# Hybrid attention and delta-rule block on one core: norm weights spread by a matrix product, squares summed on VectorE, row factors computed earlier

## The chip, the cores and the metric

The kernel runs on one core of one Trainium2 chip. The metric is the device time of one execution in microseconds (us). The time before is the median of three executions. A core has a matrix engine (TensorE, in the profile PE, with its weight loads as PEld), VectorE (DVE), ScalarE (ACT), GpSimd (POOL) and SyncE (SP), which here only issues transfers.

## The reference

One decoder layer on 1024 tokens of 1024 channels, in float32. The input is normalised, projected to 9,232 columns, goes through two token mixers, and is added back.

```
def _rmsnorm(x, w):
    y = x * rsqrt(mean(x * x, axis=-1) + NORM_EPS)
    return y * w

h = _rmsnorm(x, norm_w)              # per token a factor, per channel a weight
proj = h @ w_in
... mixer A: dilated window attention, three groups, rotary positions
... mixer B: gated delta rule in chunks of 64
merged = sigmoid(gate_a) * y_a + sigmoid(gate_b) * y_b
x = x + merged @ w_out
out = _rmsnorm(x, final_norm_w)
```

The change touches only `h` of the first line, the way in which it is brought into the kernel's tiles, and the order in which this and the first two projections are done.

## The kernel before, in words

TensorE multiplies in float16. Every operand is held as two float16 parts, an upper part (`h_hi`, `whi`) and the rest (`h_lo`, `wlo`); a product is three matmuls: upper by upper, upper by rest, rest by upper. `h_hi` and `h_lo` hold the normalised input with the channel on the partitions: 8 blocks of 128 channels by 1024 tokens. ScalarE makes an upper part, VectorE then the rest. PSUM has 8 banks of 128 x 512 float32; `bank(tag, bufs)` takes one of them, with the tags "mm" (3), "S" (2), "G" (2) and "O" (1).

The start (lines 96 to 561) normalises the input and computes the first two units of 256 columns, the queries `q` and keys `k` of one attention set, at the same time. It treats the tokens in two ways:

- **Tokens 0 to 511, four row tiles `t` of 128 tokens** (`xt`, tokens on the partitions). `rstd_rows(t)` (line 443): ScalarE squares the two halves of a row tile and sums them, takes the root; VectorE inverts it. `scale_rows(t)` (453): two operations on VectorE multiply a half of the tile by the token's factor and by the norm weights, which must lie along the free axis and be the same on all 128 partitions. That is the tile `nwr` (line 102), 128 x 1024, loaded from memory ready-made (114). `turn_rows(t)` (458): eight transposes on TensorE against the identity. `split_rows` (464): ScalarE and VectorE write the two parts into `h_hi` and `h_lo`. `rows_product(ps, w, t, c)` (471): 24 matmuls of 128 columns for one row tile and one half of the channels, a "run of rows" in what follows.
- **Tokens 512 to 1023, two quarters of 256 tokens** (`xs[2]` the third, `xs[3]` the fourth; channels on the partitions). `add_squares` (398): ScalarE squares pieces of 128 x 512, and GpSimd adds them up (`eng = GP`): three additions of 128 x 512 and one of 128 x 256 for a quarter. `rstd(i, acc)` (411): TensorE sums over the partitions, ScalarE takes the root, VectorE inverts and puts the factors on a diagonal (`diag`, two 128 x 128 blocks). `spread(i)` (421): a product of ones with the diagonal puts each token's factor on all partitions, in PSUM. `scale_x` (426): four operations on VectorE for a half of the channels, times norm weight (`nw16`, one value a partition) and factor. `split_h` (431): upper part on ScalarE, rest on VectorE. `quarter` (437): 24 matmuls of 256 columns for one block of 128 columns and one quarter.

The identity and the norm weights with one value a partition are the first 136 columns of the constants `cons`, which have a transfer of their own (116). All first loads are issued on SP's queue, in the order in which they are written (lines 112 to 116, then 483 to 492): x of row tile 0, the norm weights, the constants, the weight blocks of q, row tiles 1 and 2, the other constants, the weight blocks of k, row tile 3, the two quarters.

What sets the order: TensorE executes in the order of the program text throughout. In the block from line 495 to 559 VectorE and ScalarE also keep the order in which their instructions are written, among themselves. A scheduler may put instructions of later lines between them; it does so with the copies of `q` and `k` out of PSUM (`rope_evict`, line 599, "rx" in the profile), with the rotary products that follow (`rope_half`, 603) and with a small split (904). After the block `rope_first` (from line 656) goes on with the third quarter for `k` and the fourth for `q` and `k`. The block's second half before the change is shown at the end of this section, from line 526.

Of the kernel before, what the change touches and what calls it, by code (L numbers as in the profile page):

```python
# [19 lines left out]
D = 1024  # L20
# [57 lines left out]
def hybrid_block(ctx: ExitStack, tc: tile.TileContext, A):  # L78
# [3 lines left out]
    def STT(out, in0, scalar, in1, op0, op1, eng=None):  # L82
        (eng or V).scalar_tensor_tensor(out, in0, scalar, in1, op0=op0, op1=op1)  # L83
# [15 lines left out]
    spr = start[1].enter_context(tc.tile_pool(name="startr", bufs=1, side="right"))  # L99
    xt = sp.tile([128, 4, D], F32, name="xt")  # L100
    xs = {i: spr.tile([128, KT, 256], F32, name=f"xs{i}") for i in (2, 3)}
    nwr = spr.tile([128, D], F32, name="nwr")

    def load_xt(t, c):
        cs = slice(512 * c, 512 * c + 512)
# [2 lines left out]
    def load_x(i):  # L108
        for c in range(2):
            nc.sync.dma_start(out=xs[i][:, 4 * c:4 * c + 4], in_=A["xT"][i - 2, :, 4 * c:4 * c + 4])  # L110

    for c in range(2):
        load_xt(0, c)
    nc.sync.dma_start(out=nwr, in_=A["nwr"])
    cons = base.tile([128, A["cons"].shape[1]], F32, name="cons")
    nc.sync.dma_start(out=cons[:, :128 + KT], in_=A["cons"][:, :128 + KT])
    off = [0]

    def part(n):
# [276 lines left out]
    diag = base.tile([128, 2, 128], F32, name="diag", tag="diag", bufs=1)  # L396

    def add_squares(i, acc, c):
        eng = GP
        for k in (4 * c, 4 * c + 2):  # L400
            dst = acc if k == 0 else sp.tile([128, 2, 256], F32, name="sq", tag="sq", bufs=2)
            SC.activation(dst, xs[i][:, k:k + 2], AF.Square)
            if k:
                TT(acc, acc, dst, ALU.add, eng)
        if c:
            TT(acc[:, 0], acc[:, 0], acc[:, 1], ALU.add, eng)
# [24 lines left out]
    def split_h(i, c, n=4):  # L431
        for k in range(4 * c, 4 * c + 4, n):
            x, hl = xs[i][:, k:k + n], [h[:, k:k + n, i * 256:i * 256 + 256] for h in (h_hi, h_lo)]
            SC.copy(hl[0], x)  # L434
            TT(hl[1], x, hl[0], ALU.subtract)
# [7 lines left out]
    def rstd_rows(t):  # L443

        for c in range(2):
            junk = sp.tile([128, 2, 256], F32, name="sq", tag="sq", bufs=2).rearrange("p a b -> p (a b)")
            SC.activation(junk, xt[:, t, 512 * c:512 * c + 512], AF.Square, accum_out=ss[:, 2 * t + c:2 * t + c + 1])
        s0, s1 = ss[:, 2 * t:2 * t + 1], ss[:, 2 * t + 1:2 * t + 2]
        SC.activation(s0, s0, AF.Identity, bias=epsc, scale=1.0 / D)
        SC.activation(s1, s1, AF.Sqrt, bias=s0, scale=1.0 / D)  # L450
        V.reciprocal(s1, s1)

    def scale_rows(t):
        for c in range(2):
            x, n = xt[:, t, 512 * c:512 * c + 512], nwr[:, 512 * c:512 * c + 512]
            STT(x, x, ss[:, 2 * t + 1:2 * t + 2], n, ALU.mult, ALU.mult)

    def turn_rows(t):
        pts = [bank("G", 2), bank("G", 2)]
# [35 lines left out]
    with tc.manual_schedule(engines={nc.vector.engine, nc.scalar.engine}):  # L495
        wq, wk = w_first
        q, k = qk
        rstd_rows(0)
        scale_rows(0)
        pts = turn_rows(0)  # L500
        V.tensor_scalar(wq[0][:, 0:4], stage[0], W_SCALE, None, op0=ALU.mult)
        split_rows(0, pts, (0,))
        w_lo(stage[0], *wq, 0)
        split_rows(0, pts, (1,))
        rows_product(q, wq, 0, 0)
        w_hi(stage[1], wq[0], 1)
        w_lo(stage[1], *wq, 1)
        rows_product(q, wq, 0, 1)
        for t in (1, 2):
            rstd_rows(t)  # L510
            scale_rows(t)
        pts = turn_rows(1)
        split_rows(1, pts)
        rows_product(q, wq, 1, 0)
        pts = turn_rows(2)
        rows_product(q, wq, 1, 1)
        w_hi(stage[2], wk[0], 0)
        w_lo(stage[2], *wk, 0)
        split_rows(2, pts)
        w_hi(stage[3], wk[0], 1)  # L520
        w_lo(stage[3], *wk, 1)
        rstd_rows(3)
        scale_rows(3)
        for c in range(2):
            rows_product(q, wq, 2, c)
        for t in range(2):
            rows_product(k, wk, t, 0)
        pts = turn_rows(3)
        acc = [new_acc(0), new_acc(1)]
        for i in (2, 3):  # L530
            for c in range(2):
                add_squares(i, acc[i - 2], c)
            if i == 2:
                split_rows(3, pts)
        for t in range(2):
            rows_product(k, wk, t, 1)
        rstd(2, acc[0])
        for c in range(2):
            rows_product(k, wk, 2, c)
        pb = spread(2)  # L540
        scale_x(2, pb, 0)
        split_h(2, 0)
        for c in range(2):
            rows_product(q, wq, 3, c)
        rstd(3, acc[1])
        scale_x(2, pb, 1)
        split_h(2, 1)
        for c in range(2):
            rows_product(k, wk, 3, c)
        pb = spread(3)  # L550
        for c in range(2):
            scale_x(3, pb, c)
            split_h(3, c)
        V.tensor_copy(hide_b, hide64)
        V.tensor_copy(ident_b, ident)
        V.tensor_scalar(cw, convw, 0.5 * P_SCALE, None, op0=ALU.mult)
        q = [bank("mm", 3), bank("O", 1)]
        for ct in range(2):
            quarter(q[ct], wq, ct, 2)
# [1379 lines left out]
def _layout(x, norm_w, w_in, conv_w, a_log, dt_bias, gdn_norm_w, w_up_a, w_up_b, w_out, final_norm_w):  # L1939
    c = np.ascontiguousarray  # L1940
    x, w_in = np.asarray(x)[0], np.asarray(w_in)[0]
    cons, tabs, amask = _constants()
    rows = lambda v: np.broadcast_to(np.asarray(v).reshape(1, -1), (128, np.asarray(v).size))
    cons = np.concatenate([
        np.eye(128, dtype=np.float32),
        np.asarray(norm_w)[0].reshape(KT, 128).T,
        cons,
        np.asarray(conv_w)[0].reshape(4, 12, 128).transpose(2, 1, 0).reshape(128, 48),
        rows(np.asarray(a_log)[0]),
        rows(np.asarray(dt_bias)[0]),  # L1950
        np.tile(np.asarray(gdn_norm_w)[0], 2).reshape(128, 1),
    ], axis=1)
    wk = w_in.reshape(KT, 128, -1)
    w = np.stack([wk[:, :, cols].transpose(1, 0, 2) for cols in _columns()])
    up = np.concatenate([np.asarray(w_up_a)[0], np.asarray(w_up_b)[0]], axis=0)
    unit = lambda m: m.reshape(KT, 128, 4, 256).transpose(2, 1, 0, 3)
    return {
        "xT": c(x.T.reshape(KT, 128, 4, 256).transpose(2, 1, 0, 3)[2:]),
        "x": c(x),
        "cons": c(cons),  # L1960
        "nwr": c(rows(norm_w)),
        "tabs": tabs,
        "amask": amask,
        "w": c(w),
        "w7": c(np.stack([_seven(w[u]) for u in SEVENS])),
        "w_ba": c(wk[:, :, 7168:7184].transpose(1, 0, 2)),
        "w_up": c(unit(up)),
        "w_out": c(np.asarray(w_out)[0].reshape(2, 4, 128, 2, 512).transpose(1, 2, 0, 3, 4).reshape(4, 128, 4, 512)),
        "fnw": c(rows(final_norm_w)),
    }  # L1970
# [15 lines left out]
```

## Time and profile before

| | |
|---|---|
| median of 3 executions | 1087.89 us (1086.54, 1087.89, 1089.79) |
| span of the profiled execution | 1083.1 us |
| mean granted TensorE clock | 0.996 |
| busy PE, DVE, ACT, POOL | 1052.6, 854.9, 559.6, 66.5 us |

The time of the profiled execution itself is not listed; its span goes from the first to the last instruction and lies 4.8 us under the median. In ten-microsecond windows of the opening (busy time of each engine with its number of instructions, the granted clock, the share of the transfer engines, GB/s):

```
0.00:10.00 10.00, 2.30 (x12) 1.88 (x13) 2.83 (x8) 4.32 (x10) 0.20 (x4) 1.00 0.76 249
10.00:20.00 10.00, 8.57 (x109) 7.65 (x108) 9.32 (x15) 8.24 (x20) 0.68 (x1) 1.00 0.89 292
20.00:30.00 10.00, 10.00 (x172) 9.99 (x170) 4.58 (x7) 7.26 (x17) 6.77 (x7) 1.00 0.66 259
30.00:40.00 10.00, 10.00 (x156) 9.61 (x154) 5.70 (x13) 5.42 (x8) 3.24 (x3) 1.00 0.28 100
40.00:50.00 10.00, 8.15 (x59) 6.38 (x57) 8.77 (x14) 3.49 (x5) 0.57 (x1) 0.83 0.19 62
50.00:60.00 10.00, 10.00 (x95) 8.96 (x93) 7.25 (x12) 3.56 (x4) 0.00 (x0) 1.00 0.00 0
```

The columns are PE, PEld, DVE, ACT and POOL. TensorE's busy time counts a matmul from its start to its modelled end, and matmuls overlap. A line such as "L86" names a line of the kernel; L83 and L86 are two helpers (`STT` and `TT`) through which most of VectorE's work goes, so the tile names tell the operations apart.

### The profile page before, as it was taken

How to read it: one execution, taken by the hardware profiler on the slowest of the kernel's cores; microseconds unless marked ns; L12 is line 12 of the kernel's file. 1: busy time of each engine (PE TensorE's matmuls, PEld its weight loads, DVE VectorE, ACT ScalarE, POOL GpSimd, SP SyncE). 2: the span in 40 equal slices, each digit the busy share in tenths (PEclk: the TensorE clock that was granted, in tenths of full speed). 3: DMA queues.
4: the chain of work that ended last, by engine and by line, in shares of the span. 5: the costliest groups of instructions: out<-in, count | busy, mean ns of one | idle time of the engine just before them, and what ended most of it. 6: DMA issues, size and time to landing. Idle time of an engine off the chain costs nothing.

```text
span 1083.1 us, 23724 instructions
## 1 busy us (share of the span) xinstructions
PE 1052.6 (97%) x9426; PEld 641.4 (59%) x9426; DVE 854.9 (79%) x1967; ACT 559.6 (52%) x1272; POOL 66.5 (6%) x115
## 2 busy tenths in 40 slices
PE   6999999999999999999999999999999999999997
PEld 6894595775966855765645544555545554444443
DVE  5697897878879778979965797976588778799934
ACT  6445766667666565557645534244454345333622
POOL 1200000000000000000000000110200000000000
PEclk9999999999999999999999999999999999999999
DMA  8135531632724431741233457785685523753232
GB/s 295 60 98 136 128 109 55 167 99 66 190 79 132 101 126 47 182 117 59 75 122 136 111 130 175 250 247 159 195 269 167 147 99 101 285 185 123 83 120 78
DMA packets 99632, 148.99 MB, mean 138 GB/s; under 512 B 31152, under 2 KB 64432, under 8 KB 98368
## 3 DMA queue, kind: packets, MB, share of 16 engines
q1 hardware_dynamic: 69264, 85.20, 27.3%
q0 software_dynamic: 12320, 44.11, 13.5%
q10 hardware_dynamic: 17936, 18.16, 4.9%
q8 instruction: 74, 1.21, 0.5%
q14 instruction: 38, 0.31, 0.1%
HBM read 91.66 MB, written 36.90 MB: 119 GB/s over the span
## 4 chain that ended last, share of the span: by engine, by line
PE 59%; DVE 26%; DMA 5%; ACT 4%; issue 3%; SPq 2%; ACTq 0%; DVEq 0%
PE ps_mm L182 14%; PE ps_mm L184 14%; PE ps_mm L183 14%; DVE ca L83 4%; DVE wlo L83 2%; DVE X L86 2%; DVE stmp L86 2%; DVE sm L794 2%; DVE rt L86 2%; PE ps_S L182 1%; PE ps_S L184 1%; PE ps_S L183 1%; DVE tl L86 1%; PE ps_G L808 1%; SPq L624 1%
## 5 line engine op out<-in xcount | busy, mean ns | idle before, releaser
L184 PE MATMUL ps_mm<-h_hi,wlo 128*128 128x512 f16 (+1 forms) x552 | 208.6, 378 | 1.2 <-issue 1.2
L183 PE MATMUL ps_mm<-h_lo,whi 128*128 128x512 f16 (+1 forms) x492 | 185.9, 378 | 1.0 <-DVE h_lo L86 1.0
L182 PE MATMUL ps_mm<-h_hi,whi 128*128 128x512 f16 (+1 forms) x492 | 186.0, 378 | 0.9 <-ACT h_hi L434 0.9
L184 PEld LDWEIGHTS <-wlo 128*128 128x128 f16 x788 | 77.5, 98 | 89.5 <-issue 3.4
L182 PEld LDWEIGHTS <-whi 128*128 128x128 f16 x848 | 83.4, 98 | 70.8 <-issue 0.5
L183 PEld LDWEIGHTS <-whi 128*128 128x128 f16 x848 | 83.4, 98 | 69.1 <-issue 2.2
L182 PE MATMUL ps_mm<-whi,h_hi 128*128 128x256 f16 x384 | 105.1, 274 | 0.0
L798 ACT ACTIVATE sm<-sm,osb 128x128 f32<-128x128 f32 (+1 forms) x160 | 69.5, 435 | 68.7 <-DVE osb L794 62.0
L184 PE MATMUL ps_mm<-whi,h_lo 128*128 128x256 f16 x384 | 104.7, 273 | 0.0
L183 PE MATMUL ps_mm<-wlo,h_hi 128*128 128x256 f16 x384 | 104.7, 273 | 0.0
L86 DVE TENSOR_TENSOR tl<-ps_G,th 128x256 f16<-128x256 f32 (+1 forms) x96 | 51.8, 540 | 21.5 <-ACT th L813 21.0
L794 DVE CUSTOM_DVE_ANT_0 sm<-ps_S,amask 128x128 f32<-128x128 f32 (+1 forms) x192 | 59.2, 345 | 8.5 <-PE ps_S L787 8.3
L83 DVE SCALAR_TENSOR_TENSOR wlo<-wstage,whi 128x1024 f16<-128x1024 f32 x50 | 60.8, 1218 | 4.4 <-ACT whi L165 4.1
L83 DVE SCALAR_TENSOR_TENSOR ca<-xc,cw,ca 128x512 f32<-128x512 f32 x72 | 53.7, 746 | 7.1 <-ACT ca L1001 6.3
L165 ACT ACTIVATE whi<-wstage 128x1024 f16<-128x1024 f32 x49 | 51.3, 1051 | 3.0 <-PE ps_O L183 1.4
L83 DVE SCALAR_TENSOR_TENSOR whi<-wstage,whi 128x512 f16<-128x512 f32 x60 | 40.8, 687 | 13.6 <-ACT whi L329 12.9
L808 PE MATMUL ps_G<-cons,sm 128*128 128x128 f32 x280 | 47.5, 275 | 2.1 <-ACT sm L798 1.0
L183 PEld LDWEIGHTS <-h_hi 128*128 128x128 f16 x384 | 45.8, 119 | 1.6
L329 ACT ACTIVATE whi<-wstage 128x512 f16<-128x512 f32 x60 | 37.1, 626 | 18.5 <-DVE wstage L328 13.4
L182 PE MATMUL ps_mm<-h_hi,wlo 128*128 128x512 f16 x120 | 45.6, 380 | 1.0 <-DVE rx L83 1.0
L182 PEld LDWEIGHTS <-h_hi 128*128 128x128 f16 x384 | 45.5, 119 | 1.5
L184 PEld LDWEIGHTS <-h_lo 128*128 128x128 f16 x384 | 45.5, 119 | 1.5
(436 smaller groups left out, 2584.4 us busy)
## 6 DMA issues: line engine op xcount, KB each, us to landing
wstage<-in_w POOLq DMA_DIRECT2D x68, 512.0 KB, 4.8
og<-osb ACTq DMA_DIRECT2D x32, 132.0 KB, 2.2
og<-og SPq DMA_DIRECT2D x32, 132.0 KB, 2.2
gspb<-gst ACTq DMA_DIRECT2D x16, 256.0 KB, 2.3
sga<-gspa SPq DMA_DIRECT2D x8, 512.0 KB, 6.9
wstage<-in_w_up POOLq DMA_DIRECT2D x8, 512.0 KB, 5.1
wos<-in_w_out SPq DMA_DIRECT2D x8, 512.0 KB, 5.4
sgb<-gspb SPq DMA_DIRECT2D x8, 512.0 KB, 5.9
```

Source lines behind the costliest of these rows:

```text
L83: (eng or V).scalar_tensor_tensor(out, in0, scalar, in1, op0=op0, op1=op1)
L86: (eng or V).tensor_tensor(out, in0, in1, op)
L165: in_turn(SC.activation(hi[:, 4 * c:4 * c + 4], st, AF.Copy, scale=W_SCALE))
L182: PE.matmul(out, lhsT=wh(k), rhs=mh(k), start=first and i == 0, stop=False, skip_group_check=True)
L183: PE.matmul(out, lhsT=wh(k), rhs=ml(k), start=False, stop=False, skip_group_check=True)
L184: last_pe[0] = PE.matmul(out, lhsT=wl(k), rhs=mh(k), start=False, stop=last and i == len(ks) - 1, skip_group_check=True).ins.name
L329: in_turn(SC.activation(t[:, b, 0], self.part[name], AF.Copy, scale=W_SCALE))
L624: nc.sync.dma_start(out=dst[r0:r0 + 32, hd], in_=pt[name[1]][32 * hd:32 * hd + 32, "AB".index(name[0])])
L794: V.tensor_tensor_reduce(P[:, u, :128 * nk], psc[:, u * 256:u * 256 + 128 * nk], mask, -cexp, -NEG, ALU.add, ALU.min, accum_out=osb[:, 256 ...
L798: SC.activation(P[:, u, :128 * nk], P[:, u, :128 * nk], AF.Exp, bias=osb[:, 256 + hd:257 + hd], scale=-1.0, accum_out=osb[:, 260 + hd:261 ...
L808: PE.transpose(pt[:, c:c + 128], P[:, u, i * 128:i * 128 + 128], ident)
```

## The change

Three things are changed, all in the start.

1. The norm weights are not loaded as a tile of 128 equal rows. The constants (identity and one weight a partition) are loaded first and on ScalarE's queue. VectorE multiplies the identity by the weights (`nwd`, eight diagonal blocks), and TensorE multiplies a tile of ones by it, which gives the weights on all partitions in two PSUM banks; `scale_rows` reads them there.
2. The sums of squares of the third and fourth quarter are added on VectorE instead of GpSimd.
3. In the block's second half the order of TensorE, VectorE and ScalarE is rewritten: the factors of the third quarter are made after one run of rows of `k` (before: two), those of the fourth ahead of the last runs of rows of `q` (before: behind them), and the third quarter is scaled as a whole before the fourth's factors and split as a whole behind them.

```
-    nwr = spr.tile([128, D], F32, name="nwr")
+    nwd = spr.tile([128, KT, 128], F32, name="nwd")
+    ones0 = spr.tile([128, 128], F32, name="ones0")
+    V.memset(ones0, 1.0)
...
+    cons = base.tile([128, A["cons"].shape[1]], F32, name="cons")
+    nc.scalar.dma_start(out=cons[:, :128 + KT], in_=A["cons"][:, :128 + KT])
     for c in range(2):
         load_xt(0, c)
-    nc.sync.dma_start(out=nwr, in_=A["nwr"])
-    cons = base.tile([128, A["cons"].shape[1]], F32, name="cons")
-    nc.sync.dma_start(out=cons[:, :128 + KT], in_=A["cons"][:, :128 + KT])
...
     def add_squares(i, acc, c):
-        eng = GP
+        eng = V
...
     def scale_rows(t):
         for c in range(2):
-            x, n = xt[:, t, 512 * c:512 * c + 512], nwr[:, 512 * c:512 * c + 512]
-            STT(x, x, ss[:, 2 * t + 1:2 * t + 2], n, ALU.mult, ALU.mult)
+            x = xt[:, t, 512 * c:512 * c + 512]
+            STT(x, x, ss[:, 2 * t + 1:2 * t + 2], nwr[c], ALU.mult, ALU.mult)
...
         q, k = qk
+        TT(nwd, ident[:, None, :].to_broadcast([128, KT, 128]), normw[:, :, None].to_broadcast([128, KT, 128]), ALU.mult)
+        nwr = [bank("mm", 3), bank("O", 1)]
+        for c in range(2):
+            PE.matmul(nwr[c], lhsT=ones0, rhs=nwd[:, 4 * c:4 * c + 4].rearrange("p a b -> p (a b)"), start=True, stop=True)
         rstd_rows(0)
...
         acc = [new_acc(0), new_acc(1)]
-        for i in (2, 3):
-            for c in range(2):
-                add_squares(i, acc[i - 2], c)
-            if i == 2:
-                split_rows(3, pts)
-        for t in range(2):
-            rows_product(k, wk, t, 1)
+        for c in range(2):
+            add_squares(2, acc[0], c)
+        split_rows(3, pts)
+        rows_product(k, wk, 0, 1)
         rstd(2, acc[0])
         for c in range(2):
-            rows_product(k, wk, 2, c)
+            add_squares(3, acc[1], c)
+        rows_product(k, wk, 1, 1)
         pb = spread(2)
         scale_x(2, pb, 0)
-        split_h(2, 0)
+        rows_product(k, wk, 2, 0)
+        scale_x(2, pb, 1)
+        rows_product(k, wk, 2, 1)
+        rstd(3, acc[1])
+        for c in range(2):
+            split_h(2, c)
         for c in range(2):
             rows_product(q, wq, 3, c)
-        rstd(3, acc[1])
-        scale_x(2, pb, 1)
-        split_h(2, 1)
+        pb = spread(3)
         for c in range(2):
             rows_product(k, wk, 3, c)
-        pb = spread(3)
         for c in range(2):
             scale_x(3, pb, c)
             split_h(3, c)
```

More of the change, by code (lines that the diff above doesn't have):

```diff
@@ L1960, in _layout @@
         "cons": c(cons),
-        "nwr": c(rows(norm_w)),
         "tabs": tabs,
```

## The prediction

> **What bounds the kernel now.** I read the page first, then the waits of the opening 45 us, then the timeline of two places, then windows around the second.
>
> ```profile
> span 1083.1 us, 23724 instructions
> PE 1052.6 (97%) x9426; PEld 641.4 (59%) x9426; DVE 854.9 (79%) x1967; ACT 559.6 (52%) x1272; POOL 66.5 (6%) x115
> ```
>
> TensorE is the bound, idle for only 1083.1 - 1052.6 = 30.5 us. An edit of the opening counts only by what it does to TensorE's own idle or slow time, and what it saves there stays saved as long as TensorE's later waits move along. The waits of the first 45 us (engine, line, whom it waited for; total, times, longest):
>
> ```profile
> PE ps_G L461 <- DVE xt L83: 8.1, 2, 7.7
> PE ps_mm L183 <- DVE h_lo L86: 1.0, 1, 1.0
> PE ps_mm L477 <- DVE h_lo L83: 1.0, 1, 1.0
> PE ps_mm L182 <- ACT h_hi L434: 0.9, 1, 0.9
> ```
>
> Two places: the start, up to 7.7 us, and a hole of 0.9 + 1.0 us at some later point. The change touches both. The start in the timeline (start, duration, engine, line, tile; in brackets the idle time before and what ended it):
>
> ```profile
> 0.74 0.86 SPq L106 DMA_DIRECT2D xt<-in_x  x2
> ...
> 3.43 0.63 ACT L447 ACTIVATE sq<-xt 128x512 f32<-128x512 f32 x1 [1.20 <-DMA xt<-in_x]
> 6.14 0.16 DVE L451 RECIPROCAL ss<-ss 128x1 f32<-128x1 f32 x1 [5.24 <-ACT ss L450]
> 6.88 0.75 DVE L83 SCALAR_TENSOR_TENSOR xt<-xt,ss,nwr 128x512 f32<-128x512 f32 x1 [0.57 <-DMA nwr<-in_nwr]
> 7.54 0.16 DVE L147 TENSOR_SCALAR nw<-cons 128x8 f32<-128x8 f32 x1
> 7.62 0.74 DVE L83 SCALAR_TENSOR_TENSOR xt<-xt,ss,nwr 128x512 f32<-128x512 f32 x1
> 7.68 1.97 PE L461 MATMUL ps_G<-cons,xt 128*128 128x128 f32 x8 [7.68 <-DVE xt L83]
> 8.91 0.69 DVE L501 TENSOR_SCALAR whi<-wstage 128x1024 f16<-128x1024 f32 x1 [0.55 <-DMA wstage<-in_w]
> ...
> 17.04 0.61 PE L477 MATMUL ps_mm<-h_lo,whi 128*128 128x128 f16 x8 [0.98 <-DVE h_lo L83]
> ...
> 17.93 1.04 PE L461 MATMUL ps_G<-cons,xt 128*128 128x128 f32 x8
> ```
>
> The row factor is ready at 6.14 + 0.16 = 6.30, but the first scaling starts at 6.88: 0.57 us are lost to the loaded norm weights, and 0.55 us more to the first weight block at 8.91. The first eight transposes take 1.97 us, the same eight at 17.93 take 1.04: TensorE begins at about half speed. From 17.04 on it runs without a hole until the second place:
>
> ```profile
> 22.56 1.41 DVE L83 SCALAR_TENSOR_TENSOR xt<-xt,ss,nwr 128x512 f32<-128x512 f32 x2
> ...
> 23.45 4.35 POOL L86 TENSOR_TENSOR xt<-xt,sq 128x512 f32<-128x512 f32 x3 [0.75 <-ACT sq L402]
> ...
> 26.78 1.29 DVE L83 SCALAR_TENSOR_TENSOR h_lo<-ps_G,h_hi 128x512 f16<-128x512 f32 x2 [2.81 <-ACT h_hi L468]
> ...
> 28.57 4.03 POOL L86 TENSOR_TENSOR xt<-xt,sq 128x512 f32<-128x512 f32 x3
> ...
> 32.67 0.73 POOL L86 TENSOR_TENSOR xt<-xt 128x256 f32<-128x256 f32 x1
> ...
> 35.33 0.56 PE L414 MATMUL ps_G<-cons,xt 128*128 128x1 f32 x4
> ...
> 35.93 0.26 ACT L417 ACTIVATE rr<-ps_G,epsc 128x2 f32<-128x2 f32 x1 [0.34 <-PE ps_G L414]
> ...
> 36.09 1.97 ACT L599 COPY rx<-ps_mm 128x512 f32<-128x512 f32 x2
> ...
> 36.95 0.42 DVE L86 TENSOR_TENSOR diag<-cons,rr 128x256 f32<-128x256 f32 x1
> ...
> 37.30 1.65 DVE L83 SCALAR_TENSOR_TENSOR xs<-xs,nw,ps_G 128x256 f32<-128x256 f32 x4
> ...
> 38.43 0.65 PE L423 MATMUL ps_G<-diag,cons 128*128 128x256 f32 x2
> ...
> 38.91 0.27 PE L182 MATMUL ps_mm<-h_hi,whi 128*128 128x256 f16 x1
> ...
> 40.14 1.05 ACT L434 CAST h_hi<-xs 128x1024 f16<-128x1024 f32 x1
> ...
> 41.23 1.22 DVE L86 TENSOR_TENSOR h_lo<-xs,h_hi 128x1024 f16<-128x1024 f32 x1 [2.28 <-ACT h_hi L434]
> ...
> 47.99 0.27 PE L182 MATMUL ps_S<-h_hi,whi 128*128 128x256 f16 x1
> ...
> 53.23 0.27 PE L182 MATMUL ps_mm<-h_hi,whi 128*128 128x256 f16 x1
> ```
>
> The 48 matmuls of the query columns on the third quarter start at 38.91, the next 48 (key columns) at 47.99, the next at 53.23. The same work took 9.08 us and then 5.24 us, so the hole costs 3.84 us, not 1.9. Its cause: the upper half of the third quarter is scaled on VectorE (37.30) only after the factors of the fourth, and ScalarE copies q and k out of PSUM (36.09 and after) before it splits that half (40.14); VectorE's rest follows at 41.23. The other half of the cost is clock (busy time per engine and count, the granted clock, DMA):
>
> ```profile
> 39.19:42.60 3.41, 1.56 (x13) 1.11 (x12) 1.37 (x2) 2.21 (x4) 0.00 (x0) 1.00 0.28 115
> 42.60:46.01 3.41, 3.41 (x18) 2.42 (x18) 3.41 (x7) 1.04 (x1) 0.57 (x1) 0.50 0.10 18
> 104.07:107.48 3.41, 3.41 (x13) 1.48 (x11) 1.50 (x5) 1.44 (x8) 0.00 (x0) 0.50 0.00 0
> ```
>
> After a stretch with TensorE busy 1.56 of 3.41 us the clock is 0.50 for 3.41 us, which costs 1.71 us. So the hole is 3.84 - 1.71 = 2.13 us of waiting and 1.71 us of slow clock.
>
> **The change, part by part.** *Norm weights by a product.* Removed: a 512 KB load and two issues on SP (weights and constants), so the weight blocks behind them are issued about 0.9 us earlier. The constants now go out first, on ScalarE's queue, ahead of a table load and a tiny activation, which have room: ScalarE's first real work is at 3.43. Added: VectorE's memset and one 128x1024 product with the identity (the 128x1024 TENSOR_TENSOR at 41.23: 1.22 us), both in VectorE's 5.24 us of idle time; two f32 products of 512 columns on TensorE. From the 128x256 product at 38.43 to the next matmul is 0.48 us, so 512 columns cost some 0.9 us, and at the cold start twice that, about 1.8.
>
> When the constants land, no row shows. The nearest is the first block of x, issued in the same place and landed by 3.43; the far bound is the same constants on SP:
>
> ```profile
> cons<-in_cons SPq DMA_DIRECT2D x1, 68.0 KB, 4.8
> ```
>
> that is, 0.74 + 4.8 = 5.5. I take 3.4, since the block of x has the same position at the head of a queue. Then 3.4 + 0.16 + 1.22 = 4.8, the first product done at about 6.65, the second at 8.4. The first scaling starts at 6.65 instead of 6.88, but the second at 8.45 instead of 7.62, and VectorE's queue is in order: the weight rounding queued behind it (8.91 now) goes at about 9.2, whatever the earlier landing of the weights. TensorE is warm sooner, by about 8.5, so the transposes of the second half take half the time, and ScalarE's split of it stays in its place within 0.1. From there VectorE's chain to 17.04 is unchanged. I estimate the start at +0.2 us: the two waits of 0.57 and 0.55 are gone, and the second product is late in their place. Bounds: -0.6 (products in time; then the transposes limit) to +2.2 (landing at 5.5).
>
> *Sums on VectorE.* Removed from POOL: two sets of 4.35 or 4.03 us plus 0.73. Added to VectorE: six 128x512 additions and two of 128x256.
>
> ```profile
> L86 DVE TENSOR_TENSOR rt<-rt,rx 128x512 f32<-128x512 f32 x4 | 2.6, 688 | 0.0
> 29.62 2.70 PE ps_S L477 x48
> ```
>
> (a group by shape with its mean in ns; and a piece of the chain: two runs of rows take 2.70 us, one 1.35.) Issued back to back an addition takes about 0.65, so a quarter costs 3 x 0.65 + 0.4 = 2.35 us instead of about 5, in VectorE's idle time between 24 and 41. The first sum is queued ahead of the split of the last rows (26.78); it runs from 23.97 to about 26.4, before that split can start, so it delays nothing.
>
> *Factors ahead of other runs.* The new order, followed at these durations without the start's shift:
> - the third quarter's sum at 26.4; its factor on TensorE at 27.75 (behind one run of rows), ScalarE 0.6 later as between 35.33 and 35.93, VectorE's diagonal done by 29.4;
> - the spreading product at 29.5; the fourth quarter's sum on VectorE until about 32.0; then both halves of the third quarter's scaling, 2 x 1.65, until 35.3; the fourth's reciprocal and diagonal until 36.0;
> - TensorE meanwhile: two runs to 32.65, the fourth's factor to 33.05, two runs to 35.75; then it waits for the diagonal: 0.3 us, the one wait added, with the last runs of rows queued behind it;
> - spread to 36.5, two runs to 39.25. The third quarter's splits: ScalarE at 33.75 and 35.35, VectorE's rests done at 37.2 and 38.4, so both halves stand before 39.25, and the 48 matmuls run in 5.24.
>
> The key columns thus start at 39.25 + 5.24 = 44.5 instead of 47.99: -3.5; with +0.2 from the start -3.3. If q is copied out ahead of the upper half's split (2 x 0.98), that half is whole at about 40.1, and its first matmul is due after 12 of the 48, at 39.25 + 5.24 / 4 = 40.55: still covered; with k's copies also in front (two more of the kind) the old hole is back. The fourth quarter is due two runs of 48 later, at 49.7; on VectorE two scalings of 1.65, two rests of 1.22 and two rotation steps of 1.22 between them take it from 38.4 to about 47. What is late next is this (a row of the timeline, then one of all waits):
>
> ```profile
> 58.56 1.06 ACT L165 ACTIVATE whi<-wstage 128x1024 f16<-128x1024 f32 x1 [1.38 <-PE ps_O L183]
> ```
> ```profile
> PE ps_S L787 <- DMA Ql<-Ql: 2.3, 1, 2.3
> ```
>
> That wait ends a line of weight rounding, rotations and transfers. It begins at 58.56, where ScalarE waited 1.38 us until TensorE had done with the query weights, so it moves with TensorE and the gain is kept.
>
> *How often the slow stretch counts.* The two slow stretches begin 104.07 - 42.60 = 61.47 us apart, 18 times 3.41: they lie on a grid of 3.41 us. If the grid lies elsewhere, a hole of 2.1 us can fall across a line of it with both sides more than half busy, and no slow stretch follows. The three times before spread by 3.25 us, about two such prices, so I count the first stretch at 0.6 of 1.71, that is 1.0. [...]
>
> The sum for the median: -(2.13 - 0.3) + 0.2 - 1.0 = -2.6 us. The profiled execution's own time is not listed; its span lies 4.8 us below the median of 1087.89, and I apply the difference to that: 1085.3.
>
> **The rivals.**
> 1. *The slow stretch was in every execution*: -3.3, 1084.6. For it: the profile has it. Against: the spread of the times.
> 2. *The constants land before 3 us*: the start gives up to 0.6, in all -3.2 to -3.9, about 1084.4.
> 3. *A new wait in place of the old*: VectorE's longer queue makes the fourth's diagonal late by 1.5 to 2 us instead of 0.3, or the constants land near 5.5; about -0.7, 1087.2. Against it: VectorE's additions wait on nothing but ScalarE's squares.
> 4. *Slower*: q and k are in SBUF earlier relative to VectorE, and the instruction order may put the whole rotation of both (8 operations of about 1.22, 9.8 us) ahead of the fourth quarter's scaling at 38.4. Its first half would come at about 52 instead of 49.7: a 2 to 3 us hole, 1.7 of slow clock, and another wait for the second half, +4.5 against -2.6: about +1.9, 1089.8. It decides from some 3 us of rotation put ahead. Against it: today a rotation step goes in only where VectorE waits for ScalarE.
> 5. *Nothing changes*, because VectorE or DMA sets the pace after 58 us: 1087.9. Against it: TensorE's 97%.
>
> **How the numbers follow.** Forecast 0.50, rival 1 0.17, rival 2 0.09, rival 3 0.11, rival 4 0.08, rival 5 0.05. A change of 0.3%, 3.3 us, is about what a measurement can tell. The forecast's own spread (the stretch's share from 0 to 1, the start from -0.4 to +0.6) reaches from 1084.0 to 1086.8; a quarter of it lies beyond -3.3 (0.13), with two thirds of rival 1 (0.11) and most of rival 2 (0.07). I add 0.07 for the later instruction order, which is laid out anew behind the start and may fall better as well as worse: faster 0.38; slower by 0.3% needs rival 4 at its worst or the late landing together with it, and the same later order falling worse: 0.09. The range, 1083.2 to 1088.2, leaves out rival 4 and the best of rival 2.
>
> **What would show it.** Right: no TensorE wait of 0.9 us near 41 and clock 1.00 from 40 to 47; the key columns of the third quarter starting near 44.7 and 5.24 us before the next; POOL without additions; a TensorE wait under 0.6 for the diagonal; scalings of the first rows near 6.65 and 8.45. Wrong: the second scaling before 7.6 or after 9.5, ScalarE's four copies ahead of the upper half's split, a new TensorE wait before 60 us, or the saving at 50 us gone by 110 us.

## The result, and the profile after

Twenty-two executions of each kernel (those of before include the three that were known): before 1083.88 us (1078.52 to 1089.79), after 1079.57 us (1076.72 to 1083.70). The ratio is 0.9959 [0.9947, 0.9971], that is -4.4 us with an interval from -5.7 to -3.1. The kernel is faster by 0.41%, where the forecast was -2.6 us, under 0.3%. The 1085.3 us of the forecast lie 5.7 us above the measured median for two reasons: by the medians the change gave 1.7 us more than forecast, and the median of the three known executions of before (1087.89) lay 4.0 us above the median of 22.

The profiled execution after took 1077.67 us, with a mean granted clock of 0.998. From its page:

```profile
span 1075.9 us, 23729 instructions
PE 1051.3 (98%) x9430; PEld 639.9 (59%) x9430; DVE 860.6 (80%) x1977; ACT 560.1 (52%) x1272; POOL 56.9 (5%) x107
```

The span is 7.2 us shorter; TensorE's idle time went from 30.5 to 1075.9 - 1051.3 = 24.6 us. TensorE's waits in the first 110 us (line, whom it waited for; total, times, longest):

```profile
PE ps_mm L502 <- DVE nwd L86: 5.2, 1, 5.2
PE ps_mm L478 <- DVE h_lo L83: 1.0, 1, 1.0
PE ps_mm L478 <- DVE wlo L83: 0.8, 2, 0.5
PE ps_G L813 <- ACT sm L803: 0.6, 1, 0.6
PE ps_G L462 <- DVE xt L83: 0.3, 1, 0.3
PE ps_G L424 <- DVE diag L86: 0.3, 1, 0.3
```

Both waits of the hole (0.9 and 1.0) are gone, and the wait for the diagonal has come in with its 0.3 us. But a third one is gone as well: the wait for `Ql<-Ql`, 2.3 us before. The timeline of after, at the start and at the old hole:

```profile
0.73 0.41 ACTq L115 DMA_DIRECT2D cons<-in_cons  x1
...
3.86 0.17 DVE L148 TENSOR_SCALAR nw<-cons 128x8 f32<-128x8 f32 x1 [2.84 <-DMA cons<-in_cons]
3.94 1.22 DVE L86 TENSOR_TENSOR nwd<-cons 128x1024 f32<-128x1024 f32 x1
5.21 2.07 PE L502 MATMUL ps_mm<-nwd,ones 128*128 128x512 f32 x2 [5.21 <-DVE nwd L86]
7.08 1.91 PE L502 MATMUL ps_O<-nwd,ones 128*128 128x512 f32 x2
7.32 0.75 DVE L83 SCALAR_TENSOR_TENSOR xt<-xt,ss,ps_mm 128x512 f32<-128x512 f32 x1 [1.42 <-PE ps_mm L502]
9.03 0.75 DVE L83 SCALAR_TENSOR_TENSOR xt<-xt,ss,ps_O 128x512 f32<-128x512 f32 x1 [0.96 <-PE ps_O L502]
9.69 0.69 DVE L506 TENSOR_SCALAR whi<-wstage 128x1024 f16<-128x1024 f32 x1
...
17.99 0.61 PE L478 MATMUL ps_mm<-h_lo,whi 128*128 128x128 f16 x8 [0.99 <-DVE h_lo L83]
...
25.15 2.28 DVE L86 TENSOR_TENSOR xt<-xt,sq 128x512 f32<-128x512 f32 x3
27.46 0.42 DVE L86 TENSOR_TENSOR xt<-xt 128x256 f32<-128x256 f32 x1
...
36.52 1.05 ACT L435 CAST h_hi<-xs 128x1024 f16<-128x1024 f32 x1 [0.52 <-DVE xs L83]
37.48 1.06 ACT L604 COPY rx<-ps_mm 128x512 f32<-128x512 f32 x1
...
45.59 0.27 PE L183 MATMUL ps_S<-h_hi,whi 128*128 128x256 f16 x1
...
50.84 0.27 PE L183 MATMUL ps_mm<-h_hi,whi 128*128 128x256 f16 x1
```

The constants are there at 3.86, not at 3.4; each product takes 1.9 to 2.1 us, not 1.8; so the scalings start 0.67 and 0.58 us later than forecast, and the marker at 17.99 (the first matmul that waits for a rest of row tile 1) stands 0.95 us later than in before. The sum of a quarter takes 2.28 + 0.42 us on VectorE (2.35 was forecast), ScalarE splits both halves before its first copy of q (36.52, then 37.48), and the key columns start at 45.59, 2.40 us earlier than in before, with 5.25 us to the next 48 matmuls. The granted clock there (busy times, then clock, share of the transfer engines, GB/s):

```profile
41.20:44.60 3.40, 3.40 (x33) 3.04 (x32) 3.31 (x5) 2.01 (x3) 0.53 (x1) 1.00 0.49 149
```

So of 7.2 us between the two profiles 2.4 are gained by 50 us, 2.3 by the wait that vanished near 100 us, and 1.7 by the slow stretch that followed it in before (in after the granted clock is 1.00 in every microsecond from 98 to 112). The remaining 0.8 us was not followed further.

### The profile page after: what moved, and what is told of

Read it like the earlier page. It is cut to its first block, busy times and chain, and to the rows that moved or that the text cites. A ratio compares the mean times of both kernels' runs of the same rounds, so it can differ in the third digit from the quotient of the medians.

```text
span 1075.9 us, 23729 instructions
## 1 busy us (share of the span) xinstructions
PE 1051.3 (98%) x9430; PEld 639.9 (59%) x9430; DVE 860.6 (80%) x1977; ACT 560.1 (52%) x1272; POOL 56.9 (5%) x107
## 4 chain that ended last, share of the span: by engine, by line
PE 68%; DVE 21%; ACT 5%; issue 2%; DMA 2%; SPq 1%; ACTq 0%; DVEq 0%
PE ps_mm L183 17%; PE ps_mm L185 16%; PE ps_mm L184 16%; DVE ca L83 3%; DVE wlo L83 2%; DVE sm L799 2%; PE ps_S L183 2%; PE ps_S L185 2%; PE ps_S L184 2%; PE ps_G L813 1%; DVE tl L86 1%; DVE rt L86 1%; SPq L629 1%; ACT sm L803 1%; PE ps_G L185 1%
## 5 line engine op out<-in xcount | busy, mean ns | idle before, releaser
L813 PEld LDWEIGHTS ps_G<-cons,sm 128*128 128x128 f32 x280 | 35.5, 141 | 18.9 <-ACT sm L803 4.6
```

The lines of the kernel that those rows point to most:

```text
L813: PE.transpose(pt[:, c:c + 128], P[:, u, i * 128:i * 128 + 128], ident)
```

## The experiments

Two questions were open. First, which part of the change does what. Second, why the wait for `Ql` vanished. `Qh` and `Ql` are the upper part and the rest of the rotated q; `Qh<-Qh` and `Ql<-Ql` are transfers of 512 KB inside SBUF (the second half of the partitions gets a copy of the first) at the head of the attention; `Ql<-Ql` is the last thing it waits for. Their rows, with that of the load of weights that GpSimd issues beside them (`wstage<-in_w`, 512 KB), in before and in after:

```profile
91.42 0.53 POOL L161 DMA_DIRECT2D wstage<-in_w  x1 [12.68 <-DVE wlo L83]
92.54 0.59 SPq L627 DMA_DIRECT2D Qh<-Qh  x1
95.30 0.49 SPq L627 DMA_DIRECT2D Ql<-Ql  x1
```
```profile
87.19 1.52 SPq L632 DMA_DIRECT2D Qh<-Qh  x1
88.96 0.53 POOL L162 DMA_DIRECT2D wstage<-in_w  x1 [14.23 <-DVE wlo L83]
89.66 0.49 SPq L632 DMA_DIRECT2D Ql<-Ql  x1
```

**Theory A, collision:** in before this load goes out ahead of both copies and shares the transfer engines with them; after, the copy of `Qh` goes out first. **Theory B, VectorE:** the rotations of k come sooner because VectorE has less queued in front of them, and the copies simply land earlier. Ratios are to before, from executions on the same chip.

**The parts of the change.** `e_load`: after, with the norm weights loaded as in before (part 1 undone):

```
-    nc.scalar.dma_start(out=cons[:, :128 + KT], in_=A["cons"][:, :128 + KT])
...
+    nc.sync.dma_start(out=nwr, in_=A["nwr"])
...
+    nc.sync.dma_start(out=cons[:, :128 + KT], in_=A["cons"][:, :128 + KT])
...
-            STT(x, x, ss[:, 2 * t + 1:2 * t + 2], nwr[c], ALU.mult, ALU.mult)
+            STT(x, x, ss[:, 2 * t + 1:2 * t + 2], n, ALU.mult, ALU.mult)
```

> The changed kernel with its first part undone: norm weights loaded as 128 equal rows on SP, constants behind them on SP. Order theory (the gain comes from the third quarter's hole, and further on from rotation work that gets ahead; the product costs about 1 us at the start): TensorE's wait for the last rest of row tile 1 ends near 17.0 again instead of 18.0, the key columns of the third quarter start near 44.6, no 2.3 us wait for Ql near 100; about 1 us faster than the changed kernel, ratio to before 0.9950. Load theory (the gain comes from the 512 KB and the two issues that are gone): most of the gain goes, ratio 0.999 to 1.000.

0.9937 [0.9923, 0.9951], median 1078.63. Its waits in the first 110 us:

```profile
PE ps_G L461 <- DVE xt L83: 8.0, 2, 7.8
PE ps_mm L477 <- DVE h_lo L83: 1.0, 1, 1.0
PE ps_G L808 <- ACT sm L798: 0.6, 1, 0.6
PE ps_G L423 <- DVE diag L86: 0.3, 1, 0.3
```

The hole and the wait for `Ql` are gone without the product: both come from the other two parts. The ratio is lower than that of after (0.9959), but the two intervals overlap, so that the kernel is better without the product is likely and not shown.

`e_prod`: before with part 1 alone (the hunk above the other way round).

> The kernel before with the first part alone (norm weights by a product, constants first on ScalarE's queue). Order theory: 0.9 us later at the start, the hole near 41 and the wait for Ql near 100 stay; 0 to 1 us slower, ratio 1.000 to 1.001. Load theory: ratio 0.996 to 0.997.

1.0001 [0.9981, 1.0021], 1084.89. All three waits (0.9, 1.0 and 2.2) stay.

`e_sums`: before with part 2 alone.

```
-        eng = GP
+        eng = V
```

> The kernel before with the squares' sums on VectorE alone. Order theory: the hole near 41 comes from the order of scaling, copies and split and stays at 3.8 us or 2.1 us without its slow clock; ratio 0.999 to 1.001. Sums theory (GpSimd's 5 us per quarter were what made the factors late): the hole shrinks by over 2 us, ratio 0.997.

0.9997 [0.9978, 1.0015], 1083.68. The same three waits stay.

`e_order_gp`: after with the sums back on GpSimd (the same line the other way round), so parts 1 and 3.

> The changed kernel with the sums back on GpSimd. Order theory: the fourth quarter's sum is ready near 34, so TensorE waits some 0.5 to 1 us for it ahead of the last query rows, and nothing else comes back: 0.5 us slower than the changed kernel, ratio 0.9962. Sums theory: the factors are late enough that a hole of 2 us and a slow stretch return, ratio 0.999.

0.9975 [0.9960, 0.9989], 1082.08. No wait for `Ql`, but one that was put too low:

```profile
PE ps_G L415 <- POOL xt L86: 2.1, 2, 1.7
```

TensorE waits for GpSimd's sums, 1.7 us of it for the fourth quarter at 36.39, and the key columns start at 47.94, as in before (47.99). Part 2 is what lets part 3 gain at this place: in e_sums the hole stays, here another wait takes its place. And since the key columns start no earlier than in before while the wait for `Ql` is gone, an earlier start of TensorE is not what ended that wait.

These kernels also size the start. The marker of 17 us and the start of the third quarter's key columns, in the profiles of all kernels that share a start or an order:

| start, order | marker | key columns | between |
|---|---|---|---|
| loaded, old: before | 17.04 | 47.99 | 30.95 |
| loaded, old: e_sums, e_k_first, e_sp_load | 17.55, 17.11, 17.65 | 46.84, 48.10, 47.02 | 29.29, 30.99, 29.37 |
| product, old: e_prod | 17.49 | 46.77 | 29.28 |
| loaded, new: e_load | 17.07 | 44.67 | 27.60 |
| product, new: after, its second profile | 17.99, 18.29 | 45.59, 45.89 | 27.60, 27.60 |
| product, new: e_k_last, its second profile | 17.47, 17.94 | 45.07, 45.54 | 27.60, 27.60 |

The new order takes 27.60 us in every one; the old takes 29.3, or 31.0 where the slow stretch fell on it. So the order is worth 1.7 us, or 3.4 with the stretch. The marker moves by 0.6 to 0.8 us between executions of the same start: five with the load have a mean of 17.28, six with the product (these five and e_order_gp, 18.28) 17.91. By the means the product costs 0.63 us; the single pair of profiles had shown 0.95.

The marker follows the moment at which TensorE comes to full speed. Eight matmuls of a run of rows take 1.06 us at first and 0.61 later. With the load they take 0.61 from 12.1 to 12.8 on in the three profiles with a marker of 17.0 to 17.1, and only from 14.2 and 14.5 on in the two with 17.55 and 17.65 (e_sums, e_sp_load). With the product, the second norm product takes 1.54 and 1.56 us where the marker is 17.5 (e_k_last, e_prod), and 1.91 in the other four. The column of the granted clock shows 1.00 from 4 to 18 us in before and in after; the half speed is read from these durations.

**The start made warm.** `e_warm`: after, with ten products of ones ahead of the norm product, into a bank that is then overwritten.

```
+        for _ in range(10):
+            PE.matmul(nwr[1][:, :128], lhsT=ones0, rhs=ones0, start=True, stop=True)
```

> The changed kernel with ten idle products (ones by ones, 128 columns, f32) on TensorE ahead of the norm weights' product, into the bank that the second product overwrites; they add nothing to the output. Cold theory (the product is late because TensorE starts at half speed): the two products take about 0.95 us each instead of 1.95, the first scalings start near 6.4 and 7.3 instead of 7.32 and 9.03, the wait for the rest of row tile 1 ends 1 us or more earlier than 18.0; 1 to 1.5 us faster than the changed kernel, ratio to before 0.9945. Landing theory (the constants' landing and VectorE's chain set it): under 0.3 us, ratio 0.996.

0.9938 [0.9918, 0.9958], 1076.79. Its timeline:

```profile
5.48 1.73 PE L504 MATMUL ps_mm<-nwd,ones 128*128 128x512 f32 x2
7.05 1.02 PE L504 MATMUL ps_O<-nwd,ones 128*128 128x512 f32 x2
7.25 0.75 DVE L83 SCALAR_TENSOR_TENSOR xt<-xt,ss,ps_mm 128x512 f32<-128x512 f32 x1 [1.15 <-PE ps_mm L504]
8.11 0.75 DVE L83 SCALAR_TENSOR_TENSOR xt<-xt,ss,ps_O 128x512 f32<-128x512 f32 x1
```

The second product takes 1.02 instead of 1.91 us, the second scaling starts at 8.11 instead of 9.03, and the key columns at 44.61, 0.98 us earlier than in after. The first product still took 1.73 us, so the first scaling came at 7.25 and not at 6.4. The late second product was a matter of TensorE's speed: idle products alone moved the marker to 17.01, where the starts with the load have theirs.

**Theory B.** `e_k_first`: before, with the rounding of the rotated k (`pkh`, from which `Ks` is copied) put ahead of the next weights and copies on ScalarE, as after has it (an order among the instructions, set in `w_hi` and `rope_evict`).

```
-            SC.copy(dst[0], src)
+            halves.append(SC.copy(dst[0], src))
...
+        if len(halves) == 2:
+            tc.add_manual_dep(i.ins, halves[1].ins.name, order_only, reason="in turn")
```

> The kernel before with one order fixed: ScalarE rounds the keys' first rotated half (pkh) ahead of the next weights and of the third copy out of PSUM, as it does in the changed kernel; SP's order stays that of before. Hole theory (TensorE's earlier start alone ended the wait for Ql near 100): the wait of 2.3 us stays, ratio 1.000. VectorE theory (that order lets VectorE fill its 1.5 us gap near 58, so that the pieces of the next set are ready 1.2 us earlier): the wait falls to about 1.1 us, ratio 0.9985. Queue theory (SP's order of the pieces is what counts): 2.3 us stay.

1.0010 [0.9993, 1.0027], 1084.64. The rounding moved (VectorE's part from 62.59 to 59.33), the first piece of `Qh` went out at 68.72 as before (68.77), and the wait of 2.3 us stayed. In this form theory B falls. The copy of `Ql` itself went out 2.7 us earlier than in before (92.64) and landed no earlier (102.8).

`e_k_last`: the reverse on after, the rounding of k behind two blocks of weights.

```
                     for n in range(2):
                         feed.units[0][1].split(n)
+                rope_half(g, pts[1], 0, xk, 0)
+                tc.add_manual_dep(halves[1].ins, splits[-1].ins.name, order_only, reason="in turn")
```

> The changed kernel with the opposite order fixed: the keys' first rotated half is rounded behind the two weight blocks, as in the kernel before, whereby SP's order of the pieces becomes that of before too. Hole theory: no wait for Ql, ratio 0.996 as for the changed kernel. VectorE or queue theory: the wait of about 2.3 us near 98 comes back, in some executions with 1.7 us of slow clock: 3 us slower than the changed kernel, ratio 0.9985.

0.9982 [0.9964, 1.0001], 1081.69 (1078.14 to 1084.95). Its profile has no wait. A second profile of the same kernel, on another chip:

> A second look at the changed kernel with the keys' first rotated half behind the two weight blocks, whose first profile had no wait for Ql though its executions were slower than the changed kernel's. If the race of copies and loads is decided anew in each execution: a wait between 0 and 2.5 us. If that order always suffices: none, and the slower executions have another cause.

One execution of 1078.22, and here the wait is back:

```profile
97.76 0.22 PE L797 MATMUL ps_S<-Ks,Qh 128*128 128x128 f16 x1
100.27 0.22 PE L799 MATMUL ps_S<-Ks,Ql 128*128 128x128 f16 x1 [2.29 <-DMA Ql<-Ql]
```

One kernel, two executions, with the wait and without: in this order two queues run a race that does not always end the same way (whether the execution or the chip made the difference, two profiles can't tell). The issue times show which race (us; the load is the first of the fourth streamed pair of weight blocks; its second follows about 4 us later):

| kernel | load issued | Qh copy issued | Ql copy issued | Ql landed | attention's first product | wait |
|---|---|---|---|---|---|---|
| before | 91.42 | 92.54 | 95.30 | 102.6 | 100.21 | 2.3 |
| e_k_first | 91.46 | 91.66 | 92.64 | 102.8 | 100.44 | 2.3 |
| e_prod | 90.23 | 90.41 | 91.23 | 101.3 | 99.0 | 2.2 |
| e_k_last, second profile | 88.98 | 89.44 | 90.25 | 100.2 | 97.76 | 2.3 |
| e_sums | 90.30 | 89.54 | 91.79 | 101.6 | 99.15 | 2.3 |
| e_k_last | 88.54 | 87.85 | 88.76 | 96.8 | 97.3 | 0 |
| after | 88.96 | 87.19 | 89.66 | 97.6 | 97.81 | 0 |
| after, second profile | 89.25 | 87.73 | 89.76 | 97.9 | 98.11 | 0 |
| e_final (below) | 88.76 | 88.12 | 89.58 | 97.5 | 97.62 | 0 |
| e_warm | 87.97 | 87.21 | 88.66 | 96.4 | 96.83 | 0 |
| e_load | 88.04 | 85.43 | 86.88 | 92.9 | 96.89 | 0 |
| e_order_gp | 91.30 | 88.15 | 89.61 | 95.6 | 100.2 | 0 |
| e_best (below) | 89.18 | 87.10 | 88.59 | 95.0 | 98.04 | 0 |

The attention comes 8.8 to 9.0 us after the load in all thirteen, so the race is run against the load. Where the load is ahead, `Ql` lands 11.1 to 11.4 us behind the load, which is too late. Where the copy of `Qh` is ahead by 0.6 us or more and that of `Ql` at most 0.8 behind the load, it lands 8.2 to 8.7 behind, just in time. Where both are ahead it lands 4.3 to 5.8 behind, with time to spare. e_sums is the case in between: `Qh` ahead, `Ql` 1.5 behind, and late.

**Theory A.** `e_sp_load`: before, with nothing changed but the queue and place of this one pair of loads: SP, ordered behind the two copies.

```
...
-        (eng or nc.gpsimd).dma_start(out=st, in_=src[:, 4 * c:4 * c + 4])
+        i = (eng or nc.gpsimd).dma_start(out=st, in_=src[:, 4 * c:4 * c + 4])
+        if len(loads) == 4:
+            tc.add_manual_dep(i.ins, copies[1].ins.name, order_only, reason="in turn")
...
-                    self.st = [load_w(self.src, c) for c in range(2)]
+                    loads.append(self)
+                    self.st = [load_w(self.src, c, eng=nc.sync if len(loads) == 4 else None) for c in range(2)]
...
```

> The kernel before with one thing moved: the two loads of the fourth streamed weight unit are issued on SP behind the copies Qh and Ql of the first attention set, not on GpSimd's queue beside them. Start, third quarter and all later orders of ScalarE and VectorE are those of before. Collision theory (the wait of 2.3 us for Ql near 100 is there because the copies and these loads, 512 KB each, share the transfer engines): the copy of Ql lands some 5 us after its issue instead of 7 to 10, no wait for it, the hole near 41 stays; 2.3 us and a share of 1.7 us of slow clock, ratio 0.997. Late-pieces theory (the pieces come out of VectorE too late whatever else runs): the wait stays, ratio 1.000.

0.9970 [0.9951, 0.9989], 1081.14: -3.3 us. The hole is untouched (its two waits are 0.9 and 1.0); the issues and the attention's first products in its timeline:

```profile
90.71 0.59 SPq L631 DMA_DIRECT2D Qh<-Qh  x1
91.69 0.49 SPq L631 DMA_DIRECT2D Ql<-Ql  x1
92.35 3.69 SPq L162 DMA_DIRECT2D wstage<-in_w  x2
...
99.24 0.22 PE L789 MATMUL ps_S<-Ks,Qh 128*128 128x128 f16 x1
99.30 0.22 PE L791 MATMUL ps_S<-Ks,Ql 128*128 128x128 f16 x1
```

The wait is gone from before itself. The copies also went out earlier than in before, but that is not what did it: in e_sums the copy of `Ql` went out at 91.79 and the attention began at 99.15, as here at 91.69 and 99.24, and it landed at 101.6 instead of 97.6. The time that the transfers of `Ql` took from issue to landing, from the tile's view between 60 and 105 us; the last number is the large copy. Before, after, and this kernel:

```profile
DMA to landing us min/median/max: 1.9/3.1/7.3
```
```profile
DMA to landing us min/median/max: 2.0/2.0/7.9
```
```profile
DMA to landing us min/median/max: 1.9/2.0/5.9
```

And before's transfer engines while its copies were under way (the last three columns are the granted clock, their share and GB/s):

```profile
96.00:100.00 4.00, 4.00 (x21) 1.76 (x18) 3.62 (x4) 0.28 (x1) 0.09 (x1) 1.00 1.02 201
```

They are busy for the whole of it. Theory A stands: the order of the load and the two copies is what decides, and it is worth 2.3 us and what the clock adds.

**Versions that might beat both.** `e_best`: the norm weights loaded in two halves, the constants on ScalarE's queue, and row tile 2 scaled behind the split of tile 1.

```
+    for c in range(2):
+        nc.sync.dma_start(out=nwr[:, 512 * c:512 * c + 512], in_=A["nwr"][:, 512 * c:512 * c + 512])
...
         split_rows(1, pts)
+        scale_rows(2)
...
```

> The changed kernel with the norm weights loaded again, in two halves on SP behind x, the constants on ScalarE's queue, and the scaling of row tile 2 put behind the split of row tile 1 on VectorE. The first scaling at 6.3 to 6.5, the wait of 1.0 us for the rest of row tile 1 gone or at most half; TensorE 0.6 to 1.2 us earlier from 18 on than with the norm weights loaded as before; ratio to before 0.9930. If the loads only trade places (the first weight block later), ratio 0.9940.

0.9953 [0.9935, 0.9971], 1078.00, a miss. The first scaling came at 6.00, but then:

```profile
9.45 0.69 DVE L502 TENSOR_SCALAR whi<-wstage 128x1024 f16<-128x1024 f32 x1 [1.38 <-DMA wstage<-in_w]
...
13.61 1.06 PE L478 MATMUL ps_mm<-h_lo,whi 128*128 128x128 f16 x8
```

VectorE waited 1.38 us for the weight block, and TensorE stayed at half speed until 15 us: eight matmuls took 1.06 instead of 0.61 us. e_sp_load, whose start is that of before, stayed there until 14.5, so this need not come from the edit. The key columns started at 45.82.

`e_final`: e_load with 15 products of ones at the start and the same move of the scaling.

> The changed kernel with the norm weights loaded as before, fifteen idle products of ones on TensorE ahead of the first transposes (they add nothing to the output), and the scaling of row tile 2 behind the split of row tile 1. Cold theory: the first transposes take 1.04 us instead of 1.97, the wait of 1.0 us for the rest of row tile 1 goes; 0.6 to 1.5 us faster than with the norm weights loaded and nothing else, ratio to before 0.9925. If VectorE's chain sets the start whatever the clock: no faster, ratio 0.9937.

0.9955 [0.9937, 0.9973], 1079.70. The transposes were faster (1.39 for eight instead of 1.97), but the norm weights landed at 7.2 and the weight block held VectorE up for 0.97 us; the key columns started at 45.40. The lowest ratios are those of e_load and e_warm, some 2 us under after; their intervals overlap with that of after, and the idle products together with the loaded weights gave nothing more.

A second profile of after:

> A second look at the changed kernel itself: no wait for Ql if its lead of the copies over the loads holds in each execution; a wait of up to 2.5 us if it is close.

One execution of 1083.32 us without a wait for `Ql`. It lost its time near 740 us, where TensorE waited 2.0 us for a transfer (`MT<-u_d`) and 2.1 us more on issue, and ran at a granted clock of 0.50 for 6.8 us from 741.5 on. The first profile has neither wait; where they come from is open.

## Why the prediction was right or wrong

**Right.** The hole at 41 us was read rightly: its cause, the wait that would replace it (0.3 forecast, 0.3 measured), the order that ScalarE would fall into, the runs of 5.24 us, and its size: -1.8 forecast, -1.7 from the table. The sums on VectorE took 2.7 us a quarter instead of 2.35, and no wait of TensorE came from it beyond the 0.3 for the diagonal. One rotation step (40.98, 1.22 us) came between the two scalings of the fourth quarter and none ahead of the first, so the slower rival did not come.

**Wrong: "so it moves with TensorE and the gain is kept".** The prediction named the wait for `Ql` as what is late next, followed it to ScalarE's weight rounding at 58.56, and let it move with TensorE. That rounding is only one end of it. What made it late was a transfer of another queue, and whether that went first was a matter of 1 to 2 us. In after SP issues its first piece of `Qh` 88.96 - 65.12 = 23.84 us ahead of the load, before 22.65, and it goes from that piece to the large copy in 22.07 us instead of 23.77. Together 2.9 us, and the copies pass the load. e_load, e_order_gp, e_prod and e_sums point to part 3: it is there without part 1 and without part 2, and neither of these does it alone (part 3 alone, and parts 1 and 2 together, were not run). All seven profiles with part 3 and no other order of the k roundings are free of the wait, all four with the old order and the load on GpSimd have it. Which of its operations sets SP's order is open: e_k_first and e_k_last each moved one, and neither turned it round for good. The row that should have given it away was there: 2.3 us for a transfer named in the wait; the prediction read neither its issue and landing nor its neighbours on the other queue. Without this wait and its slow stretch the change would have given -1.8 us by the sums below, less than the 2.6 forecast: that the measured gain is larger than forecast is no merit of the terms that were forecast.

**Mis-sized: the start.** +0.2 was forecast, +0.63 came, by the means of the table. The constants at the head of ScalarE's queue are there at 3.86 and not at 3.4 (x itself came 0.25 us later than in before: 3.68 against 3.43), and the products take 2.07 and 1.91 us and not 1.8 each. TensorE was warm sooner, but not by 8.5: the second product, from 7.08, still took 1.91 us (1.02 in e_warm), and the first run of rows went at full speed from 10.53 on (eight matmuls in 0.61 us), where in before full speed came at 12.1.

**The slow stretch.** It was counted at 0.6 of 1.71 us for the hole. Of five profiles with the hole, two have it (before, e_k_first) and three do not, among them e_sums, with the same waits:

```profile
39.42 0.27 PE L182 MATMUL ps_mm<-h_hi,whi 128*128 128x256 f16 x1
...
46.84 0.27 PE L182 MATMUL ps_S<-h_hi,whi 128*128 128x256 f16 x1
```

The 48 matmuls took 7.42 us there and 9.08 in before. The prediction's reason, where the grid lies, fits e_sums if the spacing of the two stretches in before (61.47 us) holds there, which is an estimate: its slow stretch near 103 begins at 102.74 and not at 104.07, and 18 steps of 3.41 us back from there the grid parts the hole at 41.30 (busy times, then the granted clock, share of the transfer engines, GB/s; the last row is the slow stretch itself):

```profile
37.89:41.30 3.41, 3.01 (x36) 2.56 (x34) 1.57 (x5) 3.06 (x4) 0.00 (x0) 1.00 0.68 281
41.30:44.71 3.41, 1.96 (x17) 1.61 (x17) 2.97 (x7) 0.76 (x3) 0.00 (x0) 1.00 0.00 0
44.71:48.12 3.41, 3.41 (x33) 3.06 (x32) 3.41 (x7) 0.91 (x1) 0.53 (x1) 1.00 0.47 144
102.74:106.15 3.41, 3.41 (x12) 1.48 (x11) 1.72 (x7) 1.66 (x8) 0.00 (x0) 0.50 0.00 0
```

TensorE was busy for 3.01 and 1.96 of 3.41 us on the two sides, and no slow stretch followed; in before it was 1.56 on one side, and one did. That the grid lies differently from one execution to the next was the author's estimate; the profiles do not speak against it, since the same waits of 0.9 and 1.0 us led to a slow stretch in before and e_k_first and to none in e_sums, e_prod and e_sp_load. No run shows the share of 0.6 for the hole either: it was an estimate from the spread of three times, and the profiles gave two of five, 0.4. The one behind the wait for `Ql` is there in three of five (before, e_sums, e_k_first; not in e_prod or the second profile of e_k_last). Five profiles are few, and the sum is made after the result, but it fits: the hole -1.7, the wait for `Ql` -2.3, the start +0.6, slow stretches -1.71 x (0.4 + 0.6) = -1.7, together -5.1 us, within the interval from -5.7 to -3.1. The same terms give -1.7 - 2.3 - 1.7 = -5.7 for e_load (measured -6.8, from -8.3 to -5.3) and -2.3 - 1.71 x 0.6 = -3.3 for e_sp_load (measured -3.3).

**The level.** This step made most of the error in the time: the prediction applied its difference to 1087.89, the median of three, and its range allowed nothing for that median. With 22 executions it is 1083.88. Of the 5.7 us between 1085.3 and 1079.57, 4.0 are this and 1.7 the change; from 1083.88 the same range would reach from 1079.2 to 1084.2, and the result lies just inside. The 4.8 us between span and median had most of this in them: in the profiled execution of after only 1077.67 - 1075.9 = 1.8 lie between span and time.

## What to carry to other kernels

When the last wait on a path is for a transfer, list what the other queues issue in the 10 us before it: here a shift of 1.15 us turned their order round (in e_k_last the copy of `Qh` went out 0.69 us ahead of the load in one execution and 0.46 behind it in the other), and the loss was that of the whole collision, a wait of 2.3 us, not that of the shift. Put the rival on the same queue and order it behind the transfer, as e_sp_load did: there the wait of 2.3 us was gone, in the one profile taken. And take the size of a term that depends on clock or landing from several executions: single profiles of one start differed here by 0.6 to 0.8 us, as much as the term itself. The same holds for the level: three executions lay 4 us beside the median of 22.

## What the runs showed of the hardware

- The second of two 512 KB copies inside SBUF landed 5.9 to 6.4 us after its issue with no weight load in front of it (e_sp_load, e_load, e_order_gp, e_best), 7.9 with a load between the two copies (after), and up to 10.2 behind one (e_k_first). In before, where it went out 2.7 us later than in e_k_first, it took 7.3 and landed 11.2 us behind the load, there 11.4. How the engines share themselves among the three transfers is open.
- Ten idle products of 128 x 128 at the start, which add nothing to the result, bring TensorE to full speed early enough to take 0.9 us off the second norm product (1.91 to 1.02).
- When TensorE comes to full speed varies between executions of one start: 12.1 us in before, 14.5 in e_sp_load, by the time that eight matmuls take (1.06 or 0.61 us). The column of the granted clock shows 1.00 there in before.
- TensorE busy 1.56 and 1.25 of 3.41 us was followed by 3.41 us at a granted clock of 0.50 (before, from 42.60 and from 104.07); 1.96 of 3.41 was not (e_sums).
- The time of one kernel varies by 11 us over 22 executions (before), more than twice what this change gives.
